# Weight sums of the seven-product pairs made ahead of the output and down projections and parked in DRAM, in a float32 decoder trunk

## Chip, cores and metric

One core of a Trainium2 chip runs the whole program. The metric is the device time of one execution in microseconds; lower is better. The engines are TensorE (PE: matmuls, with its weight loads as PEld), VectorE (DVE), ScalarE (ACT), GpSimd (POOL) and SyncE (SP); DMA transfers are issued on the queues of SP, ACT and POOL.

## What is computed

256 tokens of width 2048 go through two decoder layers in float32. The first layer mixes tokens by gated linear attention with four heads, the second by causal attention with 16 heads over one shared key and value; a gated feed-forward with a short convolution follows each. Cut to what matters:

```python
# layer 0
q, k, v, g = split(rms_norm(x) @ w_in)                       # 2048 -> 1024, 1024, 2048, 2048
h = x + (rms_norm(gla(q, k, v, decay)) * silu(g)) @ gla_w_out      # "go": 2048 x 2048
# each layer's feed-forward
a, u = split(causal_conv3(rms_norm(h) @ w_up) + conv_b)            # "up": 2048 x 11264
h = h + (silu(a) * u) @ w_down                                     # "dn": 5632 x 2048
# layer 1
k, v = split(rms_norm(h) @ kv_w);  q = rms_norm(h) @ w_q           # "kk", "kv", "mq"
h = h + softmax_attention(q, k, v, rel_bias) @ moba_w_out          # "mo": 2048 x 2048
```

All weights together are some 411 MB of float32, each read once.

## The kernel before

**Products in three parts.** A float32 product is made of three matmuls: each operand is split into a rounded high part and a low part (`whi`, `wlo` of the weights), and high x high, high x low and low x high are accumulated. So each weight piece of 128x1024 is cast by ScalarE (`whi`, line 132) and subtracted by VectorE (`wlo`, line 133) before TensorE can use it.

**The weight stream.** `WeightStream` holds all weights in the order of use as chunks of 128x2048 (1 MiB), each read by one DMA on SP's queue into one of three raw buffers (`wraw`, line 95), and as halves of 128x1024. A step of the program takes one half (`step`, `get`); `prefetch` splits two to five halves ahead, into three pairs of buffers with some more from a pool of 34 general slots. A raw buffer is free for the chunk three later when its last split is done. Jobs beside the stream are queued with `after(steps, job)` and run when that step comes. From the code so recorded a scheduler, which models the engines in time, sets the order of each engine's instructions; every engine then works its own list strictly in order.

**Projections.** `gemm_tok` makes 512 columns for 256 tokens in eight steps of twelve matmuls (lines 281 and 284). The results come out tokens by features; where features by tokens are needed, `turned` (attention) and the feed-forward's `store` and `load` write the tile to DRAM and read it back turned, on POOL's queue, and jobs some steps later use it: 6 and 7 steps after for keys, queries and gates, 6 and 8 for the convolution (`convolve`).

**Output and down projections.** `down` serves go, dn0, mo and dn1. Each works in two column groups of 1024, over pairs k of 256 input rows (8 in go and mo, 22 in dn). A pair is a 2x2 block product. Done plainly it takes eight block products, so 24 matmuls in two steps. A seven-product pair (marked `+` in `ORDERS`) takes seven, so 21 matmuls in four steps, with sums of the input blocks (`combine`, `combs`) and of the weight blocks. Those weight sums, tiles `t` of two times 128x1024, are made by `_sums` on VectorE when the pair's chunk has come, and then split like any other half:

```python
        V.tensor_sub(t13, src[:, 512:1536], src[:, 0:1024])
        V.tensor_add(t24[:, :512], t13[:, 512:], src[:, :512])
        V.tensor_sub(t24[:, 512:], src[:, 1536:], t24[:, :512])
```

Pairs behind the `|` in `ORDERS` form the tail of a column group: they are run once for each half of its columns. After the last seven-product pair the partial sums are gathered (`c`, lines 718 to 722), four accumulating DMAs add the old rows to them (`c<-x_tok`, `c<-rows`, line 724), and after each half of the tail VectorE adds the tail's products (line 733). Finished blocks are stored, and turned by TensorE transposes (`back`, line 757) into the next stage's operand `xw`; `TURNS` says in which tail pair.

41 pairs are seven-product pairs: 4 in go, 16 in dn0, 4 in mo, 17 in dn1.

Of the kernel before, what the change touches and what calls it, by code (L numbers as in the profile page):

```python
# [27 lines left out]
FT = F // 128  # L28
# [9 lines left out]
def _order(text):  # L38
# [7 lines left out]
    "go": [_order("0 1+ 2 3+ 4 | 5 6 7"), _order("0 2 1+ 3+ 4 | 5 6 7")],  # L46
    "dn0": [_order("0 2 4 6 1+ 8 3+ 10 5+ 12 7+ 14 9+ 16 11+ 17 13+ 18 15+ | 19 20 21"),
            _order("0 2 4 6 1+ 8 3+ 10 5+ 12 7+ 14 9+ 16 11+ 17 13+ 18 15+ 19 | 20 21")],
    "mo": [_order("0 2 1+ 3+ 4 | 5 6 7"), _order("0 2 1+ 3+ 4 | 5 6 7")],
    "dn1": [_order("0 2 4 6 1+ 8 3+ 10 5+ 12 7+ 14 9+ 16 11+ 17 13+ 18 15+ | 19 20 21"),  # L50
            _order("0 1+ 2 3+ 4 5+ 6 7+ 8 9+ 10 11+ 12 13+ 14 15+ 16 17+ 18 | 19 20 21")],
# [3 lines left out]
TURNS = ((0, (1, 2)), (0, (1, 2)), (1, (0, 1)), (1, (0, 1)), (1, (1, 2)), (1, (1, 2)))  # L55


class WeightStream:
# [4 lines left out]
    def __init__(self, tc, raw, parts):  # L63
# [4 lines left out]
        self.cuts, self.lead, self.deep = {}, {}, set()  # L68
        self.sums, self.slot, self.first = {}, None, None

    def add(self, w, g, cols):
        for c0 in range(0, cols, 2048):
            n = min(2048, cols - c0)
            for o in range(0, n, 1024):
                self.halves.append((len(self.chunks), o, "plain"))
            self.chunks.append((w, g, c0, n))

    def add_quads(self, w, g, order, deep):

        first = len(self.halves)  # L80
        for i, (_, seven) in enumerate(order[0]):
            c = len(self.chunks)
            self.halves += ([(c, 0, "b11"), (c, 1024, "wide"), (c, 0, "t13"), (c, 0, "t24")] if seven else
                            [(c, 0, "wide"), (c, 1024, "wide")])
            self.chunks.append((w, g, 2048 * i, 2048))
        if deep:
            self.deep.update(range(first, len(self.halves)))

    def _dma(self, upto):
        while self.n_dma < min(upto, len(self.chunks)):  # L90
            w, g, c0, n = self.chunks[self.n_dma]
            t = self.raw.tile([128, 2048], F32, name="wraw")
            for a, b in self.cuts.get(self.n_dma, ((0, n),)):
                rows = w[g, 128 * c0:128 * (c0 + n)].rearrange("(p c) -> p c", p=128)
# [6 lines left out]
    def _sums(self, c):  # L101

        V, src = self.nc.vector, self.tiles[c]
        t13, t24 = (self.slot([128, 1024], F32, k) for k in ("t13", "t24"))
# [5 lines left out]
    def prefetch(self, i):  # L110
        nc = self.nc
        while self.n_split < len(self.halves):
# [10 lines left out]
            if kind == "b11":  # L123
                src = src[:, :512]
# [938 lines left out]
```

## Time and profile before

| | us |
|---|---|
| median of 3 runs | 2235.65 (2232.77 to 2240.84) |
| the profiled execution | 2234.8 |
| its span, first to last instruction | 2233.0 |
| TensorE busy | 2192.9 (98%), 9805 matmuls |
| VectorE busy | 1585.1 (71%) |
| ScalarE busy | 1270.8 (57%) |
| GpSimd busy | 263.0 (12%) |
| DMA | 495.40 MB, mean 222 GB/s |

By the first matmul of each stage the attention projections run to 297 us of the span, go to 405, the first up projection to 885, dn0 to 1122, the cross projections (mq, kk, kv) to 1420, mo to 1512, the second up projection to 1992, and dn1 to the end. Matmuls are pipelined and one is counted as busy from its issue to its modelled end; how fast TensorE goes is seen better from the number of matmuls in a stretch than from its busy time. A line of code such as 132 or 692 serves many tiles, so rows name the tile too.

### The profile page before, as it was taken

The numbers are of one execution on the slowest core, as the hardware profiler recorded it, in microseconds if no ns is written. First come the engines' busy times: TensorE is split into PE (matmuls) and PEld (weight loads), VectorE is DVE, ScalarE is ACT, GpSimd is POOL, SyncE is SP. The second block draws the span as 40 slices with busy tenths as digits, with TensorE's granted clock in tenths as the row PEclk, the third lists the DMA queues.
The fourth block names the chain that finished last, engine by engine and source line by source line (L and its number), as shares of the span: only waits on it lengthen the run. The fifth ranks groups of instructions, "written<-read, shape, count | busy, mean of one in ns | idle before, by whom it ended". The sixth has DMA issues, their size and how long they took to land.

```text
span 2233.0 us, 26994 instructions
## 1 busy us (share of the span) xinstructions
PE 2192.9 (98%) x9805; PEld 1810.5 (81%) x9805; DVE 1585.1 (71%) x2162; ACT 1270.8 (57%) x1812; POOL 263.0 (12%) x368
## 2 busy tenths in 40 slices
PE   9999979999999999999999999999999999999999
PEld 7887857888888888788878888888888888887887
DVE  6655568577767767978856666776676767779886
ACT  6555545565655656555556666555565565655453
POOL 1011111111111111000021000011111111110000
PEclk9999999999999999999999999999999999999999
DMA  8576657777777787566685444486777777774655
GB/s 315 172 224 188 205 173 247 214 242 240 244 243 242 234 249 235 192 220 215 225 284 207 172 169 170 171 253 209 250 238 238 245 242 244 235 241 186 219 215 169
DMA packets 87238, 495.40 MB, mean 222 GB/s; under 512 B 12433, under 2 KB 12961, under 8 KB 37058
## 3 DMA queue, kind: packets, MB, share of 16 engines
q1 hardware_dynamic: 60578, 417.53, 53.9%
q0 software_dynamic: 25952, 75.59, 13.3%
q8 instruction: 76, 1.25, 0.2%
q10 hardware_dynamic: 576, 0.58, 0.1%
q14 instruction: 56, 0.46, 0.1%
HBM read 455.88 MB, written 37.77 MB: 221 GB/s over the span
## 4 chain that ended last, share of the span: by engine, by line
PE 82%; issue 12%; DMA 4%; DVE 1%; POOL 1%; ACT 0%; SPq 0%; DVEq 0%; POOLq 0%; ACTq 0%
PE acc L281 41%; PE acc L284 21%; PE acc L692 11%; PE p L692 7%; DMA c<-rows 1%; DMA wraw<-w_go 1%; DMA turned<-z 1%; DVE wlo L133 1%; POOL upT L634 0%; DMA turned<-queries 0%; PE sT L526 0%; PE o L543 0%; DMA wraw<-w_v 0%; DMA turned<-gates 0%; PE tr L849 0%
## 5 line engine op out<-in xcount | busy, mean ns | idle before, releaser
L133 DVE TENSOR_TENSOR wlo<-wraw,whi 128x1024 fp32r<-128x1024 f32 (+1 forms) x786 | 929.0, 1191 | 458.9 <-ACT whi L132 440.2
L132 ACT CAST whi<-wraw 128x1024 fp32r<-128x1024 f32 (+1 forms) x786 | 799.6, 1027 | 688.5 <-PE acc L281 435.3
L281 PE MATMUL acc<-whi,xw 128*128 128x512 f32 x3840 | 953.7, 390 | 3.6 <-ACT xw L244 1.9
L281 PEld LDWEIGHTS acc<-whi,xw 128*128 128x128 f32 x3840 | 720.8, 188 | 154.7 <-ACT xw L244 3.0
L284 PE MATMUL acc<-wlo,xw 128*128 128x512 f32 x1920 | 514.9, 389 | 0.0
L284 PEld LDWEIGHTS acc<-wlo,xw 128*128 128x128 f32 x1920 | 360.2, 188 | 74.7
L692 PE MATMUL acc<-whi,hid 128*128 128x512 f32 x572 | 185.2, 393 | 2.5 <-DVE c L733 2.5
L692 PE MATMUL p<-whi,hid 128*128 128x512 f32 x506 | 167.5, 393 | 0.0
L281 PE MATMUL acc<-whi,xkv 128*128 128x512 f32 x512 | 133.9, 394 | 0.0
L634 POOL DMA_DIRECT2D upT<-turned x176 | 114.0, 654 | 147.1 <-DMA turned<-z 64.5
L692 PE MATMUL acc<-whi,comb 128*128 128x512 f32 x328 | 109.2, 397 | 20.8 <-ACT whi L132 16.6
L692 PEld LDWEIGHTS acc<-whi,hid 128*128 128x128 f32 x572 | 108.2, 190 | 26.0 <-DVE c L733 3.4
L132 ACT CAST whi<-t 128x1024 fp32r<-128x1024 f32 x82 | 85.3, 1051 | 76.6 <-PE p L692 41.5
L628 POOL DMA_DIRECT2D turned<-z x44 | 34.1, 774 | 679.1 <-DVE z L624 633.0
L133 DVE TENSOR_TENSOR wlo<-t,whi 128x1024 fp32r<-128x1024 f32 x82 | 99.4, 1219 | 19.8 <-PE p L692 9.9
L692 PEld LDWEIGHTS p<-whi,hid 128*128 128x128 f32 x506 | 96.2, 190 | 20.3
L281 PEld LDWEIGHTS acc<-whi,xkv 128*128 128x128 f32 x512 | 94.1, 188 | 18.3
L642 ACT ACTIVATE au<-upT,cs 128x256 f32<-128x256 f32 x176 | 96.0, 595 | 15.8 <-DMA upT<-turned 15.7
L692 PE MATMUL acc<-wlo,hid 128*128 128x512 f32 x286 | 94.8, 390 | 0.0
L692 PEld LDWEIGHTS acc<-whi,comb 128*128 128x128 f32 x328 | 62.5, 191 | 35.9 <-ACT whi L132 18.4
L692 PE MATMUL p<-wlo,hid 128*128 128x512 f32 x253 | 83.8, 390 | 0.0
L724 POOL DMA_DIRECT2D c<-rows x24 | 21.3, 1100 | 520.1 <-DVE c L719 508.2
(241 smaller groups left out, 1931.2 us busy)
## 6 DMA issues: line engine op xcount, KB each, us to landing
wraw<-w_up SPq DMA_DIRECT2D x176, 1024.0 KB, 5.3
wraw<-w_dn SPq DMA_DIRECT2D x88, 1024.0 KB, 5.2
turned<-z POOLq DMA_DIRECT2D x44, 512.0 KB, 3.5
upT<-turned POOLq DMA_DIRECT2D x176, 128.0 KB, 4.9
wraw<-w_g SPq DMA_DIRECT2D x16, 1024.0 KB, 5.1
wraw<-w_go SPq DMA_DIRECT2D x16, 1024.0 KB, 6.1
wraw<-w_mq SPq DMA_DIRECT2D x16, 1024.0 KB, 6.1
wraw<-w_kk SPq DMA_DIRECT2D x16, 1024.0 KB, 4.9
```

Of the source, the lines that this page charges most:

```text
L132: nc.scalar.copy(hi[:, a:b], src[:, a:b])
L133: nc.vector.tensor_sub(lo[:, a:b], src[:, a:b], hi[:, a:b].bitcast(F32))
L281: T.matmul(ps[:, t, :], xs(kt)[:, x0 + 128 * t:x0 + 128 * t + 128], hi[:, c:c + 512], start=kt == 0 and x0 == 0, stop=False)
L284: T.matmul(ps[:, t, :], xs(kt)[:, 128 * t:128 * t + 128], lo[:, c:c + 512], start=False, stop=kt == KT - 1)
L628: nc.gpsimd.dma_start(turned[J].rearrange("(a i) r q c -> (i r) a (q c)", a=4), z.rearrange("p (a q) t c -> p a (q t c)", a=4))
L634: nc.gpsimd.dma_start(f[32 * q:32 * q + 32].rearrange("p a (i c) -> p (a i) c", i=4), turned[J][:, :, q, :].rearrange("a r c -> r a c"))
L642: A.activation(au[:, i, :], t[:, i, :], AF.Identity, bias=col(cb + n), scale=col(cw + 2 * 2 * FT + n))
L692: T.matmul(p[n], x[xi], w[wi][:, 512 * f:512 * f + 512], start=n not in begun, stop=left[n] == 0)
L724: nc.gpsimd.dma_start(r[n], res(n // 2, 2 * b + n % 2), accum_op=OP.add)
```

## The change

The weight sums are no longer made in the output and down projections. While the projections run, `make_sums` starts, every few steps, a job that fetches a later chunk of a seven-product pair a second time, on POOL's queue in two halves into two general slots; four steps later VectorE makes four sums of 128x512 in place, and POOL's queue parks them in DRAM. In the down stages a seven-product pair then reads two chunks, the raw one (its halves `b11` and `wide`) and the parked sums. 14 sums are made in the attention projections (every 5 steps), 10 in the first part of each up projection (every 8), 14 in the cross projections (every 6). With that the seven-product pairs become 48: 6 in go, 18 in dn0, 6 in mo, 18 in dn1. The orders of pairs are new, and go and mo have a tail of two pairs, not three, right behind a seven-product pair.

Jobs on turned tiles, and the sums, are recorded inside `behind()`: they stand after the latest weight split on ScalarE and VectorE. The turned tiles are used one or two steps later than before.

```diff
-    "go": [_order("0 1+ 2 3+ 4 | 5 6 7"), _order("0 2 1+ 3+ 4 | 5 6 7")],
+    "go": [_order("0 2 1+ 4 3+ 5+ | 6 7"), _order("0 2 1+ 4 3+ 5+ | 6 7")],
...
-TURNS = ((0, (1, 2)), (0, (1, 2)), (1, (0, 1)), (1, (0, 1)), (1, (1, 2)), (1, (1, 2)))
+TURNS = ((0, (1, 1)), (0, (1, 1)), (1, (0, 1)), (1, (0, 1)), (1, (1, 1)), (1, (1, 1)))
...
+            self.cuts[c] = ((0, 512), (1024, 2048))
+            sums = self.parked([128, 2048])
+            self._add(sums, 2048)
+            self.unmade.append((rows, sums))
+            self.halves += [(c, 0, "b11"), (c, 1024, "wide"), (c + 1, 0, "wide"), (c + 1, 1024, "wide")]
...
-    def _sums(self, c):
...
+    def behind(self):
+        stack = ExitStack()
+        for ins in self.latest:
+            stack.enter_context(self.tc.issue_after(ins))
+        return stack
+    def fetch_blocks(self):
+        rows, sums = self.unmade.pop(0)
+        x = [self.slot([128, 1024], F32, "sums") for _ in range(2)]
+        for i in range(2):
+            self.nc.gpsimd.dma_start(x[i], rows[:, 1024 * i:1024 * i + 1024])
+        def make():
+            V = self.nc.vector
+            (b11, b12), (b22, b21) = ((t[:, :512], t[:, 512:]) for t in x)
+            with self.behind():
+                V.tensor_sub(b11, b12, b11)
+                V.tensor_sub(b12, b22, b12)
+                V.tensor_sub(b22, b22, b11)
+                V.tensor_sub(b21, b21, b22)
+            for i in range(2):
+                self.nc.gpsimd.dma_start(sums[:, 1024 * i:1024 * i + 1024], x[i])
+        return make
...
+            self.latest = [one.ins, two.ins]
...
+    def make_sums(first, count, every):
+        for i in range(count):
+            def fetch():
+                job = ws.fetch_blocks()
+                after(4, job)
+            after(first + every * i, fetch)
...
+    make_sums(24, 14, 5)
...
-        through(hd, z, [(6 + i, lambda f, c=2 * hd + i: gated(c, f)) for i in range(2)])
+        through(hd, z, [(8 + i, lambda f, c=2 * hd + i: gated(c, f)) for i in range(2)])
...
+        make_sums(2, 10, 8)
...
-                after(6 + 2 * i, lambda J=J, i=i: convolve(2 * J + i, f[J][:, 2 * i:2 * i + 2, :]))
+                after(8 + 2 * i, lambda J=J, i=i: convolve(2 * J + i, f[J][:, 2 * i:2 * i + 2, :]))
...
+    make_sums(4, 14, 6)
```

`ws.cuts` is assigned anew further down, in both kernels, so the entry for the shorter load is not in force.

What the scheduler makes of it, at three places. First ScalarE at the start of go, before; `g<-turned` (now L619) is the job on a turned gate tile, `tok<-acc` (now L630) the evacuation of the last gate projection:

```order
L132 CAST whi<-t_2307 128x1024
L132 CAST whi<-wraw 128x1024
L589 ACTIVATE g<-turned,cs 128x256 x4
L600 ACTIVATE tok<-acc,col_n 128x512 x2
L294 CAST go<-g 128x2x256
```

and after:

```order
L151 CAST whi<-wraw 128x1024 x2
L630 ACTIVATE tok<-acc,col_n 128x512 x2
L151 CAST whi<-wraw 128x1024 x2
L151 CAST whi<-wraw 128x512
L151 CAST whi<-wraw 128x1024 x2
L619 ACTIVATE g<-turned,cs 128x256 x4
L312 CAST go<-g 128x2x256 x2
```

The evacuation has moved ahead of the turned tile, with five weight pieces between them.

Second VectorE near the start of dn0, before; `t` are weight sums, `comb` and `whole` sums of inputs, `au` belongs to the convolution:

```order
L105 TENSOR_TENSOR t_7148<-wraw 128x1024
L571 TENSOR_TENSOR comb<-whole,comb 128x128
L133 TENSOR_TENSOR wlo<-wraw,whi 128x512
L649 TENSOR_TENSOR au<-au 128x256
L568 TENSOR_TENSOR comb<-whole 128x128
L570 TENSOR_TENSOR comb<-whole 128x128
L578 TENSOR_TENSOR whole<-hid 128x512
L106 TENSOR_TENSOR t_7149<-t_7148,wraw 128x512
L133 TENSOR_TENSOR wlo<-t_7148,whi 128x1024
```

and after, from the low part of a pair's last sums on:

```order
L152 TENSOR_TENSOR wlo<-wraw,whi 128x1024 x3
L152 TENSOR_TENSOR wlo<-wraw,whi 128x512
L608 TENSOR_TENSOR whole<-hid 128x512
L598 TENSOR_TENSOR comb<-whole 128x128
L600 TENSOR_TENSOR comb<-whole 128x128
L677 SCALAR_TENSOR_TENSOR au<-upT,cs,au 128x255
L152 TENSOR_TENSOR wlo<-wraw,whi 128x1024
```

The sums are gone from among the splits; the input sums and the convolution are still there.

Third TensorE at the end of go's first column group, before; `p_2409` is a product of the tail's second half of columns, `c_2572` and `c_2574` are finished row blocks that are transposed:

```order
L692 MATMUL p_2409<-whi,go 128x512 x4
L692 MATMUL p_2409<-wlo,go 128x512 x2
L692 MATMUL acc<-whi,go 128x512 x4
L692 MATMUL acc<-wlo,go 128x512 x2
L692 MATMUL acc<-whi,go 128x512 x4
L692 MATMUL acc<-wlo,go 128x512 x2
L757 MATMUL acc<-mk,c_2572 128x2x2x32
L757 MATMUL acc<-mk,c_2574 128x2x2x32
```

and after, where `p_2567` is that product, `c_2837` and `c_2839` are those blocks and `p_2960` belongs to the next group:

```order
L726 MATMUL p_2567<-wlo,go 128x512 x2
L726 MATMUL acc<-whi,go 128x512 x4
L726 MATMUL acc<-wlo,go 128x512 x2
L791 MATMUL acc<-mk,c_2837 128x2x2x32
L726 MATMUL acc<-whi,go 128x512 x4
L726 MATMUL acc<-wlo,go 128x512 x2
L726 MATMUL acc<-whi,go 128x512 x4
L726 MATMUL acc<-wlo,go 128x512 x2
L726 MATMUL acc<-whi,go 128x512 x4
L726 MATMUL acc<-wlo,go 128x512 x2
L726 MATMUL acc<-whi,go 128x512 x2
L791 MATMUL acc<-mk,c_2839 128x2x2x32
```

Between the group's last seven-product pair and its first transpose there stood an eight-product pair and most of a tail of three pairs; now there are 42 matmuls of a tail of two, and the transposes of the second block come 20 matmuls later.

More of the change, by code (lines that the diff above doesn't have):

```diff
@@ L67, in __init__, with _add @@
         self.n_dma = self.n_split = 0
-        self.cuts, self.lead, self.deep = {}, {}, set()
-        self.sums, self.slot, self.first = {}, None, None
+        self.cuts, self.lead = {}, {}
+        self.unmade, self.slot, self.parked, self.first = [], None, None, None
+        self.latest = []
+    def _add(self, rows, n):
+        self.chunks.append((rows, n))
+        return len(self.chunks) - 1
     def add(self, w, g, cols):
@@ L114, in prefetch @@
             c, o, kind = self.halves[n]
-            if n > i + self.AHEAD + (kind != "plain") + 2 * (n in self.deep):
+            if n > i + self.AHEAD + (kind != "plain"):
                 break
             self._dma(c + 1)
-            for c_, _, kind_ in self.halves[n:n + (5 if n in self.deep else 3)]:
-                if kind_ == "b11" and c_ not in self.sums:
-                    self._dma(c_ + 1)
-                    self._sums(c_)
-            src = self.sums[c][kind] if kind in ("t13", "t24") else self.tiles[c][:, o:o + 1024]
-            if kind == "b11":
-                src = src[:, :512]
-            if kind != "plain" and n % 4 == 3 or n in self.deep and n % 2:
+            src = self.tiles[c][:, o:o + (512 if kind == "b11" else 1024)]
+            if kind != "plain" and n % 4 == 3:
                 hi, lo = self.slot([128, 1024], F32R, "whi"), self.slot([128, 1024], F32R, "wlo")
@@ L177, in trunk @@
     ws = WeightStream(tc, raw, parts)
+    ws.parked = lambda shape: dram.tile(shape, F32, name=f"sums{len(ws.unmade)}")
     plan = [(w_v2, 1, 16384), (w_v, 2, 8192), (w_k, 2, 8192), (w_qa, 2, 8192), (w_g, 4, 8192), (w_go, "go", None),
@@ L184, in trunk @@
             for g, order in enumerate(ORDERS[groups]):
-                ws.add_quads(w, g, order, groups in ("go", "mo"))
+                ws.add_quads(w, g, order)
             continue
@@ L388, in through, with run @@
             after(2, lambda: got.update(f=load(g)))
+            def run(job):
+                with ws.behind():
+                    job(got["f"])
             for lag, job in jobs:
-                after(lag, lambda job=job: job(got["f"]))
+                after(lag, lambda job=job: run(job))
         return square, through
@@ L639, in convolve @@
             au = temp("au")
+            with ws.behind():
+                for i in range(2):
+                    n = i * FT + j
+                    A.activation(au[:, i, :], t[:, i, :], AF.Identity, bias=col(cb + n),
+                                 scale=col(cw + 2 * 2 * FT + n))
             for i in range(2):
                 n = i * FT + j
-                A.activation(au[:, i, :], t[:, i, :], AF.Identity, bias=col(cb + n),
-                             scale=col(cw + 2 * 2 * FT + n))
                 V.scalar_tensor_tensor(au[:, i, 1:], t[:, i, :S - 1], col(cw + 2 * FT + n), au[:, i, 1:],
```

54 lines of the change are left out of this document (21 added, 33 removed).

## Prediction

> **What bounds the kernel now.** I read the page's busy shares first, then the span in stretches of 50 us.
>
> ```profile
> span 2233.0 us, 26994 instructions
> PE 2192.9 (98%) x9805; PEld 1810.5 (81%) x9805; DVE 1585.1 (71%) x2162; ACT 1270.8 (57%) x1812; POOL 263.0 (12%) x368
> ```
>
> ```profile
> 150.00:200.00 50.00, 47.27 (x206) 39.20 (x205) 26.35 (x35) 20.84 (x27) 8.03 (x10) 0.93 0.75 216
> 300.00:350.00 50.00, 33.82 (x132) 26.38 (x132) 28.92 (x33) 22.91 (x32) 7.58 (x9) 0.86 0.55 163
> 900.00:950.00 50.00, 45.70 (x187) 36.29 (x186) 48.00 (x74) 28.57 (x37) 0.00 (x0) 0.93 0.47 171
> 1700.00:1750.00 50.00, 50.00 (x223) 41.40 (x222) 34.64 (x51) 29.59 (x42) 6.72 (x10) 1.00 0.77 249
> 2000.00:2050.00 50.00, 45.86 (x189) 36.50 (x188) 47.83 (x75) 26.94 (x37) 2.29 (x4) 0.93 0.55 191
> ```
>
> The columns are PE, PEld, DVE, ACT and POOL busy with their counts, the granted clock, the DMA share and GB/s. TensorE is the bound nearly everywhere: an undisturbed stretch (1700) holds 222 to 223 matmuls, 0.225 us each, a step of twelve 2.70 us. The count shows what the busy time hides, since matmuls at a lowered clock also count as busy: 300:350 is 90 matmuls short (20.3 us), 900:950 is 35 short (7.9 us), 2000:2050 33 short (7.4 us). These three are the start of the attention output product ("go") and of the two down projections. So a change can gain by fewer matmuls, or in these three places. The go start, in order of time:
>
> ```profile
> 305.55 1.70 ACT L589 ACTIVATE g<-turned,cs 128x256 f32<-128x256 f32 x4 [5.09 <-DMA turned<-gates]
> 307.16 1.24 ACT L600 ACTIVATE tok<-acc,col_n 128x512 f32<-128x512 f32 x2
> 308.45 1.20 PE L692 MATMUL acc<-whi,comb 128*128 128x512 f32 x4 [4.14 <-ACT tok L600]
> 327.37 1.04 ACT L132 CAST whi<-wraw 128x1024 fp32r<-128x1024 f32 x1 [7.97 <-DMA wraw<-w_go]
> 333.09 1.04 ACT L132 CAST whi<-wraw 128x1024 fp32r<-128x1024 f32 x1 [4.67 <-DMA wraw<-w_go]
> 337.25 0.80 PE L692 MATMUL acc<-whi,comb 128*128 128x512 f32 x1 [10.86 <-ACT whi L132]
> ```
>
> ScalarE sits 5.09 us on a turned tile while the evacuation (L600) that TensorE needs stands behind it. Fifteen microseconds later two weight loads are late, and TensorE waits 10.86 us. At the down projections another engine is full:
>
> ```profile
> 920.00:925.00 5.00, 1.67 (x5) 0.59 (x4) 5.00 (x10) 1.60 (x2) 0.00 (x0) 0.89 0.00 0
> 925.00:930.00 5.00, 4.46 (x11) 3.49 (x12) 5.00 (x8) 4.15 (x6) 0.00 (x0) 0.50 0.60 210
> L105 DVE TENSOR_TENSOR t<-wraw 128x1024 f32<-128x1024 f32 x3 | 3.7, 1217 | 1.6 <-DMA wraw<-w_dn 1.6
> L106 DVE TENSOR_TENSOR t<-t,wraw 128x512 f32<-128x512 f32 x3 | 2.0, 681 | 0.0
> L107 DVE TENSOR_TENSOR t<-wraw,t 128x512 f32<-128x512 f32 x3 | 2.0, 681 | 0.0
> ```
>
> VectorE is busy for all of both stretches, DMA idle in the first. The groups (busy us, mean ns of one) are those of 885:932, where 7.7 us of VectorE's work are weight sums. After the gap the clock is 0.50.
>
> **The change, part by part.** *Products.* Seven more pairs of seven save 3 matmuls each: 21 x 0.225 = 4.7 us, on the bound. **-4.7.**
>
> *Weight sums out of the down stages.* 41 times (1.2 + 0.68 + 0.68) = 105 us of VectorE leave them, 7.7 us in each of the two places where VectorE is full. What is lost there is 7.9 and 7.4 us. The convolutions now come two steps (5.4 us) later into that stretch, so I take 7 each: **-14**, bounds -15.3 and 0.
>
> *Turned work behind the latest piece.* At the go start the evacuation now stands ahead of the turned tile and that tile's job is 2 steps later, more than the 5.09 us. The two late loads followed when ScalarE and VectorE caught up and freed raw buffers together; without the first wait, and without sums in the raw buffers, most of that goes. Against it, go loads 22 pieces instead of 16 beside the last turned tiles. I take **-14** of the 20.3; bounds -20.3 and 0.
>
> *Sums in the projections.* 48 times four subtractions of 128x512 by 0.68 us are 131 us of VectorE; 192 half-piece transfers of 0.5 MiB and 48 more piece loads of 1 MiB carry 151 MB more. The first subtraction waits on VectorE for its fetch, issued four steps (10.8 us) before; behind it stand the next splits, whose pieces TensorE needs some three steps later. (The shortened load of a seven-product piece does not come about: the table of cuts is overwritten later, and the SP order still loads 2048 columns.) By stage before, and what DMA can do:
>
> ```profile
> 65.00:297.00 232.00, 229.26 (x1042) 191.06 (x1042) 136.59 (x170) 126.77 (x181) 29.83 (x38) 0.99 0.63 199
> 405.00:621.00 216.00, 216.00 (x960) 178.97 (x959) 151.29 (x222) 126.68 (x185) 31.55 (x47) 1.00 0.74 235
> 1122.00:1420.00 298.00, 296.68 (x1436) 247.16 (x1435) 195.00 (x316) 177.98 (x308) 29.98 (x31) 1.00 0.55 193
> 292.00:296.00 4.00, 4.00 (x20) 3.30 (x19) 2.01 (x2) 0.97 (x3) 0.00 (x0) 1.00 1.01 423
> 324.00:328.00 4.00, 2.38 (x11) 1.65 (x9) 0.00 (x0) 0.63 (x1) 0.00 (x0) 1.00 1.05 280
> ```
>
> Full DMA moved 423 GB/s with weights alone and 280 with turned tiles of attention beside them. The attention projections get 14 sums (29.4 MB): 199 becomes 326 GB/s, the share 0.63 becomes 0.93, VectorE 0.59 becomes 0.75. The first 216 us of each up projection get 10 (21 MB): 235 becomes 332, 0.74 becomes 0.97, VectorE 0.70 becomes 0.83. The cross projections get 14: 0.55 becomes 0.78, VectorE 0.65 becomes 0.78. So on average it fits, hidden under matmuls. In the late half of attention it does not quite: the 150:200 row's 0.75 plus 2.1 MB per five steps (13.5 us, 155 GB/s, 0.37) is 1.12. What is late then is the software queue, and behind it on POOL the turned loads and the small pow instructions:
>
> ```profile
> POOL rr L839 <- DVE ss L837: 169.5, 8, 32.6
> ACT whi L132 <- PE acc L281: 435.3, 317, 2.4
> L634 POOL DMA_DIRECT2D upT<-turned x176 | 114.0, 654 | 147.1 <-DMA turned<-z 64.5
> upT<-turned POOLq DMA_DIRECT2D x176, 128.0 KB, 4.9
> ```
>
> Until now POOL waited before each rr; now fetches and parks stand there, each park behind its subtractions on VectorE, and VectorE waits for rr. The second row is the cover: pieces mostly wait for TensorE, not TensorE for them. Cost between 0 and 12% of 147 us (18) in attention, taken 5, since the stage's mean is below full; 0 to 8 in each up projection, taken 1 each; 0 to 18 in the cross projections (8 rr, each late by one landing of 4.9 us less a step of 2.7), taken 3, near the cover's end. **+10.** POOL's own issue, 192 by 0.65 us, lies in its 88% idle time.
>
> By the Trainium skill ("DMA: Bandwidth & Descriptors", section "Where 436 GB/s comes from") memory binds HBM transfers at about 358 GB/s for a core. An estimate by that: the late half of attention, which wants 371, runs 4% over, 5 us on the sum; the 423 row stands against it, if for 4 us only.
>
> *Loads in the down stages.* A pair of seven now needs two pieces in 21 x 0.225 = 4.7 us of products, and two pieces at 423 GB/s take 5.0; a pair of eight between (one piece in 5.4 us) gives it back. Three pairs of seven stand in a row at three places, where the DMA falls 0.9 us behind before a landing of 5 us or so is counted; so 0 to 6 us, taken near the lower end: **+2.**
>
> *The shorter tail of go and mo.* This is the new wait. Before, an eight-product pair and a tail of three followed the last seven-product pair; now a tail of two follows at once. In that time the partial sums must take in the old rows by DMA:
>
> ```profile
> 339.79 0.58 ACT L718 COPY c<-acc 128x512 f32<-128x512 f32 x1 [0.18 <-PE acc L692]
> 342.24 0.94 POOL L724 DMA_DIRECT2D c<-x_tok  x1 [19.20 <-DVE c L719]
> 352.11 0.69 DVE L733 TENSOR_TENSOR c<-c,acc 128x512 f32<-128x512 f32 x1 [1.28 <-DMA c<-x_tok]
> 357.55 0.69 DVE L733 TENSOR_TENSOR c<-c,p 128x512 f32<-128x512 f32 x1 [4.75 <-DMA c<-x_tok]
> 358.53 0.60 PE L757 MATMUL acc<-mk,c 128*128 128x128 f32 x4
> c<-rows POOLq DMA_DIRECT2D x24, 256.0 KB, 8.8
> ```
>
> The last seven ended at 339.5; the first row block was whole 13.3 us later, the second 18.7, and the transposes came at 19.0, just in time. In the new order 42 matmuls (9.5 us) stand before the first transpose of the first group and 62 (14.0 us) before the second's, and 42 and 48 (10.8) in the last group, and TensorE takes them in order. Readiness as before (13.3 and 18.7) gives waits of 3.8 + 0.9 us in a first group and 3.8 + 4.1 in a last one, 25 us over go and mo, with some half-clock time behind them 28. VectorE is freer now: with issue 1.2 us after the last product, a landing of 8.8 and the addition of 0.7, the first block is ready at 10.7 and the second some 2.5 later, and the waits are 1.2 and 2.3 us, 7 in all; a quicker landing leaves 4. Between the two, nearer the lower: **+13.**
>
> Sum: -4.7 - 14 - 14 + 10 + 2 + 13 = -7.7. The profiled execution took 2234.8 us, 0.85 below the median 2235.65; from the median **2228 us**.
>
> **Rivals.** *B, the tails stay hidden:* the scheduler's places are met, because accumulates land early in a quieter software queue. For it: 8.8 us is a median, and c<-x_tok waited only 1.28 us in the first row. Then 2228 - 13 = 2215. *C, DMA is full, slower:* with fetch, park and turned tiles mixed, DMA delivers some 300 GB/s, between the 280 row and 325. Attention needs 46.2 + 29.4 MB and each up half 50.8 + 21: 219 MB at 300 take 730 us against 664 of matmuls. Late turned tiles block ScalarE and VectorE ahead of the next pieces, and up to 66 us appear there, less the 7 counted: up to 2287; at 323 GB/s it costs 15, 8 more than counted, and the gain is gone. With half of that price, since lags of 7 and 8 steps and the slack of later stages absorb a part: 2254. *D, go stays as it is:* six more pieces beside the turned gates and the last parks, so its loads are late again: 2228 + 14 = 2242.
>
> **Chances.** Forecast 0.42 (own range 2219 to 2237), B 0.24, C 0.20, D 0.14. About 0.3% (6.7 us) is what a measurement can tell from no change. The forecast lies at that edge: 0.24 of its 0.42 counts as faster, 0.18 as the same; B faster; D half same, half slower; C slower but 0.02: faster 0.48, same 0.27, slower 0.25. For the range I cut B's better end (all bounds of gain: 2195) and C's worse half: 2207 to 2254.
>
> **What would show it.** Right: 300:350 without the wait on turned gates ahead of the evacuation, VectorE below full at the start of the down projections, TensorE waits on c in the tails of go and mo, DMA above 320 GB/s in attention at an unbroken matmul count. Wrong: turned or sums tiles as releasers of ScalarE or VectorE with TensorE waiting in the projections (C), w_go or sums pieces as releasers at go (D), no wait at the transposes (B).

## The result, and the profile after

The changed kernel takes 2266.7 us in the median (2262.5 to 2270.8), the kernel before 2234.2 beside it: a ratio of 1.0141 with a 95% interval of 1.0111 to 1.0170. It is 1.4% slower and lies above the range, where 2228 had been forecast. The profiled execution took 2266.8 us. The page's first lines:

```profile
span 2265.0 us, 27747 instructions
PE 2201.1 (97%) x9784; PEld 1805.7 (80%) x9784; DVE 1626.9 (72%) x2280; ACT 1284.0 (57%) x1834; POOL 368.3 (16%) x560
```

TensorE ran 21 matmuls fewer, as forecast, and the span is 32 us longer. The stretches that answer to those of before (columns as there: PE, PEld, DVE, ACT, POOL busy with counts, clock, DMA share, GB/s):

```profile
65.00:297.00 232.00, 227.84 (x1045) 188.49 (x1043) 161.86 (x214) 126.18 (x180) 55.64 (x85) 1.00 0.90 304
150.00:200.00 50.00, 46.87 (x203) 37.39 (x202) 38.12 (x52) 26.22 (x37) 15.19 (x24) 1.00 0.98 328
411.00:627.00 216.00, 216.00 (x955) 178.69 (x955) 169.88 (x253) 124.79 (x183) 52.71 (x86) 0.99 0.96 321
1130.00:1428.00 298.00, 294.36 (x1412) 243.92 (x1411) 217.46 (x360) 173.70 (x301) 59.64 (x85) 1.00 0.80 291
300.00:350.00 50.00, 42.69 (x167) 30.50 (x166) 39.52 (x51) 28.26 (x39) 11.98 (x16) 0.97 0.90 295
907.00:957.00 50.00, 42.32 (x173) 34.03 (x173) 38.82 (x61) 27.09 (x36) 0.00 (x0) 0.90 0.68 242
2034.00:2084.00 50.00, 43.49 (x184) 35.16 (x183) 38.47 (x60) 27.14 (x36) 0.00 (x0) 0.93 0.73 257
```

The projections (first four rows) carry the making nearly unharmed. The DMA shares of the first, third and fourth row are within 0.03 of those worked out. The late half of attention (second row), for which 1.12 had been worked out, moves 328 GB/s at a share of 0.98, and TensorE does 203 matmuls there instead of 206. The starts of the down projections (last two) have VectorE at 38 of 50 us, where 48 stood before, and still hold fewer matmuls (173 and 184; before 187 and 189). TensorE's waits, in all, times, longest (us): first two rows of the kernel before, then of the changed one.

```profile
PE acc L692 <- ACT whi L132: 16.6, 3, 10.9
PE acc L692 <- DVE c L733: 2.5, 2, 1.5
```
```profile
PE acc L726 <- ACT whi L151: 21.6, 14, 5.3
PE acc L791 <- DVE c L767: 10.7, 3, 5.5
PE acc L726 <- DVE c L767: 10.2, 4, 5.4
PE acc L726 <- DVE wlo L152: 5.1, 3, 2.4
PE hf L791 <- DVE c L767: 1.7, 1, 1.7
PE p L726 <- DVE c L767: 1.2, 1, 1.2
```

Waits for c, the output sums, grew from 2.5 to 23.8 us; waits for high parts of weights became many small ones and did not go. By stage, from the first weight matmul of one to that of the next in the trace, and in dn1 to the last one (us; "cross" is its three projections; the experiments follow below):

| kernel | attention | go | up0 | dn0 | cross | mo | up1 | dn1 |
|---|---|---|---|---|---|---|---|---|
| before | 291.7 | 107.4 | 480.1 | 237.1 | 298.1 | 91.5 | 480.1 | 237.1 |
| changed | 293.2 | 111.8 | 481.5 | 237.8 | 299.2 | 105.2 | 484.5 | 241.8 |
| e1 old tails | 290.4 | 95.4 | 480.1 | 239.0 | 297.6 | 92.1 | 480.1 | 242.4 |
| e4 no making | 286.0 | 103.1 | 480.3 | 237.8 | 298.2 | 101.9 | 481.3 | 241.2 |
| e7 e1, no making | 285.9 | 95.9 | 480.1 | 236.1 | 298.6 | 90.8 | 480.1 | 250.3 |
| e8 eight behind | 291.3 | 112.5 | 481.5 | 240.9 | 300.1 | 107.2 | 481.6 | 245.0 |
| e17 earlier making | 290.8 | 100.9 | 481.5 | 239.2 | 299.6 | 104.9 | 481.8 | 245.8 |
| e5 before, new tails | 292.0 | 99.8 | 481.5 | 236.7 | 298.5 | 98.5 | 481.4 | 235.6 |
| e9 before, "behind" | 288.7 | 99.1 | 480.1 | 237.1 | 298.3 | 91.3 | 480.1 | 236.8 |
| e15 e9, late convolutions | 286.7 | 99.1 | 480.1 | 236.6 | 298.1 | 91.5 | 480.1 | 236.1 |
| e10 e1, dn order | 291.6 | 95.1 | 480.3 | 238.6 | 298.2 | 92.8 | 480.4 | 237.0 |
| e13 e10, convolutions | 289.1 | 96.3 | 480.1 | 229.4 | 301.7 | 92.6 | 480.3 | 230.9 |
| e14 e9, four parked | 286.9 | 98.9 | 480.1 | 232.9 | 298.1 | 91.4 | 480.1 | 231.7 |

The loss lies in go and mo with what follows them, and the gain expected in dn0 and dn1 is missing. The ends of the two column groups of mo, in order of time (start, us, engine, line, operation, then in brackets the idle time before it and what ended it):

```profile
1465.34 0.57 ACT L752 COPY c<-acc 128x512 f32<-128x512 f32 x1
1467.77 0.88 POOL L758 DMA_DIRECT2D c<-rows  x1 [36.25 <-DVE c L753]
1472.08 2.63 POOL L758 DMA_DIRECT2D c<-rows  x3 [3.43 <-DVE c L755]
1477.61 0.69 DVE L767 TENSOR_TENSOR c<-c,acc 128x512 f32<-128x512 f32 x1 [3.20 <-DMA c<-rows]
1478.35 2.08 PE L726 MATMUL acc<-whi,ox 128*128 128x512 f32 x4 [5.36 <-DVE c L767]
1514.62 0.58 ACT L752 COPY c<-acc 128x512 f32<-128x512 f32 x1
1523.78 0.67 DVE L767 TENSOR_TENSOR c<-c,acc 128x512 f32<-128x512 f32 x1
1532.89 0.69 DVE L767 TENSOR_TENSOR c<-c,p 128x512 f32<-128x512 f32 x1 [4.80 <-DMA c<-rows]
1533.63 0.90 PE L791 MATMUL acc<-mk,c 128*128 128x128 f32 x3 [5.54 <-DVE c L767]
```

In the first group it is the next group's first product that waits longest (its accumulators are not yet emptied), in the last group the transposes. The first row block can be added to 9 to 12 us after the copy begins, the second only 18.

### The profile page after: what moved, and what is told of

Read it like the earlier page. It is cut to its first block, busy times and chain, and to the rows that moved or that the text cites. A ratio compares the mean times of both kernels' runs of the same rounds, so it can differ in the third digit from the quotient of the medians.

```text
span 2265.0 us, 27747 instructions
## 1 busy us (share of the span) xinstructions
PE 2201.1 (97%) x9784; PEld 1805.7 (80%) x9784; DVE 1626.9 (72%) x2280; ACT 1284.0 (57%) x1834; POOL 368.3 (16%) x560
## 5 line engine op out<-in xcount | busy, mean ns | idle before, releaser
L152 DVE TENSOR_TENSOR wlo<-wraw,whi 128x1024 fp32r<-128x1024 f32 (+1 forms) x882 | 1038.7, 1190 | 482.1 <-ACT whi L151 442.6
L151 ACT CAST whi<-wraw 128x1024 fp32r<-128x1024 f32 (+1 forms) x882 | 890.1, 1026 | 755.9 <-PE acc L299 367.7
L726 PE MATMUL p<-whi,hid 128*128 128x512 f32 x488 | 161.6, 393 | 1.2 <-DVE c L767 1.2
L726 PE MATMUL acc<-whi,comb 128*128 128x512 f32 x384 | 125.2, 397 | 7.8 <-ACT whi L151 7.5
L131 POOL DMA_DIRECT2D sums<-sums x96 | 53.0, 552 | 453.1 <-DVE sums L127 304.3
L726 PEld LDWEIGHTS acc<-whi,comb 128*128 128x128 f32 x384 | 72.5, 190 | 28.1 <-ACT whi L151 13.4
L679 DVE SCALAR_TENSOR_TENSOR au<-upT,cs,au 128x254 f32<-128x254 f32 x176 | 80.9, 476 | 0.0
```

Source lines behind the costliest of these rows:

```text
L131: self.nc.gpsimd.dma_start(sums[:, 1024 * i:1024 * i + 1024], x[i])
L151: one = nc.scalar.copy(hi[:, a:b], src[:, a:b])
L152: two = nc.vector.tensor_sub(lo[:, a:b], src[:, a:b], hi[:, a:b].bitcast(F32))
L679: V.scalar_tensor_tensor(au[:, i, 2:], t[:, i, :S - 2], col(cw + n), au[:, i, 2:], op0=OP.mult, op1=OP.add)
L726: T.matmul(p[n], x[xi], w[wi][:, 512 * f:512 * f + 512], start=n not in begun, stop=left[n] == 0)
```

## Experiments

Each time is a median, each ratio against the kernel before on the same chip.

**Old tails.** go and mo get their orders of before, with two pairs of seven fewer in each of them, so 44 sums.

```diff
-    "go": [_order("0 2 1+ 4 3+ 5+ | 6 7"), _order("0 2 1+ 4 3+ 5+ | 6 7")],
+    "go": [_order("0 1+ 2 3+ 4 | 5 6 7"), _order("0 2 1+ 3+ 4 | 5 6 7")],
...
-    make_sums(24, 14, 5)
+    make_sums(24, 12, 5)
```

> The changed kernel with the go and mo orders of before: two pairs of seven in a group, an eight-product pair and a tail of three behind the last of them (44 pairs of seven and parked sums in place of 48). Theory T (the tail is the largest loss: TensorE's waits for c grew from 2.5 to 23.8 us): they go back to about 2.5, -21.3, and 12 matmuls more cost 2.7: 2266.7 - 18.6 = 2248 us. Rival R (the additions come late because the software queue is full, whatever stands behind the last pair of seven): the waits for c stay above 15 us and the time stays within 2258 to 2268.

2231.0 us, 0.9990 (0.9976 to 1.0004): 36 us less than the changed kernel, twice what T had worked out. (Two makings fewer run in the attention and two in the cross projections.) Waits for c fell to 0.3 us. mo and up1 together gave back 17.5 us, go and up0 17.8. The first half of the first up projection beside it, with ten makings:

```profile
396.00:612.00 216.00, 216.00 (x960) 178.96 (x959) 171.13 (x251) 125.00 (x174) 50.22 (x81) 1.00 0.98 326
```

DMA at 0.98 and 326 GB/s costs TensorE not one matmul: 960, as before. What up0 and up1 had lost in the changed kernel came from the tails ahead of them.

**Sums in other buffers.** Parked sums are loaded into slot buffers, not raw ones.

```diff
+            if self.n_dma in self.parts_of:
+                t = [self.slot([128, 1024], F32, "wsum") for _ in range(2)]
+                for i in range(2):
+                    self.nc.sync.dma_start(t[i], rows[:, 1024 * i:1024 * i + 1024])
...
```

> The changed kernel with the loads of parked sums going to two slot buffers of 512 KiB instead of a raw buffer, for 41 of the 48 pairs (not the last seven pairs of the first group of dn0): the three raw buffers then hold weights alone, as before the change. Theory T (a pair of seven now takes two of the three raw buffers, so a piece is asked for too late and TensorE waits 25 us for whi and wlo at the starts of go, dn0 and dn1): half to all of these waits go, 2266.7 less 13 to 25: 2242 to 2254 us. Rival R (DMA bandwidth or VectorE holds the splits there): within 3 us of 2266.7.

2265.8 us, 1.0143 (1.0126 to 1.0161): the rival's number; T fell. At the start of dn0 the pieces were there, and the wait went to the engines that split them, VectorE with splits and convolutions and ScalarE behind it:

```profile
923.49 1.21 DVE L161 TENSOR_TENSOR wlo<-wraw,whi 128x1024 fp32r<-128x1024 f32 x1
925.19 0.42 ACT L690 ACTIVATE au<-au 128x256 f32<-128x256 f32 x1 [2.90 <-DVE au L688]
926.38 1.04 ACT L160 CAST whi<-wraw 128x1024 fp32r<-128x1024 f32 x1
927.47 1.22 PE L735 MATMUL acc<-whi,hid 128*128 128x512 f32 x2 [8.43 <-ACT whi L160]
```

**Shorter loads in force.**

```diff
-    ws.cuts = {0: ((0, 512), (512, 1024), (1024, 1536), (1536, 2048))}
+    ws.cuts[0] = ((0, 512), (512, 1024), (1024, 1536), (1536, 2048))
```

> The changed kernel with the shortened load of a seven-product piece in force (its columns 512 to 1024 are not loaded): 48 times 0.25 MiB less on the hardware queue. Theory T (the late loads are a matter of when they are asked for and how long one takes): each late piece lands about 0.6 us earlier (0.25 MiB at the 423 GB/s seen), some 10 waits, so 4 to 8 us less: about 2261 us. Rival R (DMA bytes bind in the starts of go and the down projections): 10 us or more off, 2257 or below.

2275.8 us, 1.0198 (1.0173 to 1.0224): 9 us slower than the changed kernel, which neither had. The load becomes two transfers, and no smaller one lands earlier by much (median us from issue to landing at the row's end); TensorE's waits for high parts of weights rose from 21.6 to 37.5 us:

```profile
wraw<-w_dn SPq DMA_DIRECT2D x52, 1024.0 KB, 6.2
wraw<-w_dn SPq DMA_DIRECT2D x36, 512.0 KB, 6.3
wraw<-w_dn SPq DMA_DIRECT2D x36, 256.0 KB, 5.3
```
```profile
PE acc L726 <- ACT whi L151: 37.5, 27, 4.8
```

**No making.** One parked tile serves all loads of sums.

```diff
-            sums = self.parked([128, 2048])
+            self.one = getattr(self, "one", None) or self.parked([128, 2048])
+            sums = self.one
...
-    make_sums(24, 14, 5)
+    make_sums(24, 1, 5)
```

> The changed kernel without 47 of the 48 makings: no fetch of blocks, no subtractions and no park in the projections but for one; every load of sums reads that one parked tile, so all pieces and products of the down stages stay (their values are not the reference's). Theory T (the making is nearly hidden: projections lost 8.4 us against before, and the last parks 2 or 3 at the start of go): 2266.7 - 11 = 2256 us, between 2252 and 2260. Rival R (the traffic of the making, 151 MB with its queues, is the main loss, through delayed tiles): 2235 to 2245 us.

2241.3 us, 1.0035 (1.0022 to 1.0049): 25 us less than the changed kernel, so R's number. By stage attention gave 7, go 9, mo 3 and the up projections 4 us; e17 below shows that what go gives hangs on when the last parks are issued.

**The tails alone**, in the kernel before.

```diff
-    "go": [_order("0 1+ 2 3+ 4 | 5 6 7"), _order("0 2 1+ 3+ 4 | 5 6 7")],
+    "go": [_order("0 2 1+ 4 3+ 5+ | 6 7"), _order("0 2 1+ 4 3+ 5+ | 6 7")],
...
```

> The kernel before with the new orders of go and mo alone (three pairs of seven, then at once a tail of two); its weight sums stay on VectorE in the down stages, nothing is parked. Theory T1 (the tail costs by itself: waits for c of some 20 us and half-clock time behind them, less 2.7 us of products): 2234 + 22 = 2256 us. Rival T2 (the tail hurts only beside the making's traffic in the software queue and the parked pieces' loads): 2229 to 2239 us.

2238.5 us, 1.0018 (1.0001 to 1.0034): 4 or 5 us slower than the kernel before, T2's number. Yet the profile shows the tail's price there too, mo and up1 8.3 us longer, and beside it a gain of 6.2 in go and up0: the new order of go waits less for high parts of weights at its start (8.8 us in the whole kernel, where 16.6 stood). Waits for c:

```profile
PE acc L692 <- DVE c L733: 13.9, 7, 4.5
```

**Earlier convolutions**, on e1.

```diff
-                after(8 + 2 * i, lambda J=J, i=i: convolve(2 * J + i, f[J][:, 2 * i:2 * i + 2, :]))
+                after(6 + 2 * i, lambda J=J, i=i: convolve(2 * J + i, f[J][:, 2 * i:2 * i + 2, :]))
```

> e1_tail with the convolutions of the up projections back at lags of 6 and 8 steps (8 and 10 in the change); still behind the latest piece. Theory V (VectorE is full at the starts of dn0 and dn1 because the last convolutions were moved there in place of the weight sums): waits of 8.6 and 7.3 us there and the half clock behind them go, 10 to 16 us off the 2231 of e1_tail: 2215 to 2221. Rival L (the pieces themselves come too late there): within 3 us of 2231; a second rival, that earlier convolutions make ScalarE and VectorE wait for turned tiles in the projections: above 2234.

2359.8 us, 1.0563 (1.0535 to 1.0592): the second rival, 129 us slower than e1. ScalarE now stands in front of turned tiles that have not landed (first row e6, second e1):

```profile
ACT au L673 <- DMA upT<-turned: 202.5, 42, 8.8
```
```profile
L673 ACT ACTIVATE au<-upT,cs 128x256 f32<-128x256 f32 x176 | 94.4, 595 | 2.3 <-DMA upT<-turned 2.3
```

Whether this comes from the convolution's place right behind a piece or from the making's transfers beside it was not separated; the kernel before has these lags with neither.

**No making, old tails:** e1 with the edit of e4.

```diff
-    make_sums(24, 12, 5)
+    make_sums(24, 1, 5)
...
```

> e1_tail without 43 of its 44 makings (no fetches, subtractions and parks; every load of sums reads the one parked tile, so its values are not the reference's). Theory T (with the old tails the making is almost hidden: what is left is in the attention projections and the first loads of go): 2231 - 6 = 2225, between 2221 and 2229. Rival R (the making costs as much as e4_nomake against the changed kernel, 25 us, whatever the tails): 2203 to 2210.

2228.0 us, 0.9974 (0.9956 to 0.9992): T. Beside the old tails the making costs 3 us, beside the new ones 25 (e4). The 3 us are a balance: attention is 4.5 and dn0 2.9 us shorter than in e1, dn1 7.9 longer, and no run shows why. Set against e4, this run gives the price of the new tails without the making: 19.7 us in go, up0, mo and up1 together.

**An eight-product pair behind the pairs of seven**, in the changed kernel.

```diff
-    "go": [_order("0 2 1+ 4 3+ 5+ | 6 7"), _order("0 2 1+ 4 3+ 5+ | 6 7")],
+    "go": [_order("0 2 1+ 3+ 5+ 4 | 6 7"), _order("0 2 1+ 3+ 5+ 4 | 6 7")],
```

> The changed kernel with all 48 pairs of seven, but go and mo in the order 0 2 1+ 3+ 5+ 4 | 6 7: three pairs of seven in a row and the eight-product pair 4 (24 matmuls, 5.4 us) between the last of them and the tail of two. Theory T1 (the price of the tail is the time between the last pair of seven and the end of the group): each of the four waits shrinks by up to 5.4 us and the half clock with it, 2266.7 - 18 = 2249, between 2243 and 2255. Rival L (six pieces in a row come too late): 2260 or more, the waits for whi taking the place of those for c.

2268.1 us, 1.0159 (1.0137 to 1.0181): the rival's number, though not its picture: waits for high parts rose to 25.8 us, but those for c stayed at 23.4. They only moved to later blocks. TensorE hardly waits for the first block any more (0.9 us in one group of four), 1.4 to 1.7 for the second in each group, and at the ends of go and mo the first product of the next stage waits 4.9 and 5.6 for the last. The end of mo, whose gathering begins at 1514.62:

```profile
1536.14 0.69 DVE L767 TENSOR_TENSOR c<-c,p 128x512 f32<-128x512 f32 x1 [3.23 <-DMA c<-rows]
1539.10 3.40 PE L299 MATMUL acc<-whi,xw 128*128 128x512 f32 x8 [5.59 <-DVE c L767]
```

So 5.4 us more of products cover the first of the four accumulating DMAs and not the last.

**One part of the change alone:** turned tiles of attention behind the latest piece, in the kernel before.

```diff
-                after(lag, lambda job=job: job(got["f"]))
+                after(lag, lambda job=job: run(job))   # run: with ws.behind(): job(got["f"])
...
-        through(hd, z, [(6 + i, lambda f, c=2 * hd + i: gated(c, f)) for i in range(2)])
+        through(hd, z, [(8 + i, lambda f, c=2 * hd + i: gated(c, f)) for i in range(2)])
```

> The kernel before with one part of the change: in the attention projections turned tiles are worked on behind the latest weight piece, with the new lags there (7, 8, 10, 13). Up projections, weight sums on VectorE, 41 pairs and all orders stay as before. Theory T (this part alone gives what the prediction counted for it): attention as in e4_nomake, 6 us less, and the start of go 8 to 12 less: 2233.9 - 16 = 2218, between 2214 and 2222. Rival S (the gain at go came from taking the weight sums out of it): 2227 to 2236.

2220.9 us, 0.9953 (0.9938 to 0.9969): T. Attention is 3.0 and go 8.3 us shorter.

**Order at the start of the down projections**, on e1.

```diff
-    "dn0": [_order("0 2 4 1+ 6 3+ 8 5+ 10 7+ 12 9+ 14 11+ 16 13+ 18 15+ 17 | 19 20 21"),
+    "dn0": [_order("0 2 4 6 1+ 8 3+ 10 5+ 12 7+ 14 9+ 16 11+ 17 13+ 18 15+ | 19 20 21"),
```

> e1_tail with the first groups of dn0 and dn1 in the order of before (0 2 4 6 1+ 8 3+ ... in place of 0 2 4 1+ 6 3+ ...): the same 16 pairs of seven, the first of them one eight-product pair (5.4 us) later, and a tail right behind the last. Theory V (VectorE is full there with the last convolutions and the combinations for the first pairs of seven; a later first pair spreads them): the waits of 9.3 and 7.3 us at the two starts fall by half or more, 6 to 14 off the 2231 of e1_tail: 2217 to 2225. Rival L (one late piece, whatever the order): 2228 to 2234.

2223.4 us, 0.9953 (0.9936 to 0.9970): V's number, though in this profile only dn1 is shorter, by 5.4.

**Deeper look-ahead** in go and mo, in the changed kernel.

```diff
-            if n > i + self.AHEAD + (kind != "plain"):
+            if n > i + self.AHEAD + (kind != "plain") + 2 * (n in self.deep):
```

> The changed kernel with the deeper look-ahead of before in go and mo (weights split two half-pieces further ahead, with four more slot buffers in use). Theory D (go and mo lose because the change took that depth out: pieces late at the start, and splits in the way of the additions in the tail): 2266.7 less 10 to 20: 2247 to 2257. Rival (the depth doesn't matter, the landing of the accumulating DMAs does): 2262 to 2270.

2272.2 us, 1.0178 (1.0158 to 1.0197): D fell; the rival's 2262 to 2270 was missed by 2. Go and mo are 5.6 and 7.2 us longer. (The change also takes this look-ahead out of go and mo; its description above does not mention it.)

**Rows loaded ahead**, in the changed kernel.

```diff
-                        nc.gpsimd.dma_start(r[n], res(n // 2, 2 * b + n % 2), accum_op=OP.add)
+                        V.tensor_add(r[n], r[n], old[n // 2][:, n % 2])   # old: loaded two pairs earlier
```

> The changed kernel with the old rows of go and mo loaded into two slot buffers two pairs before the last pair of seven, and added by VectorE (four additions of 0.68 us a group) in place of the accumulating DMAs: no landing of 9 us stands between the last pair of seven and the tail. Theory T (that landing sets the waits for c, 23.8 us, and the half clock behind them, 8): 2266.7 - 28 = 2239, between 2234 and 2246. Rival R (the additions themselves are late, behind splits on a full VectorE, or late pieces take their place): 2255 or more.

2253.2 us, 1.0094 (1.0079 to 1.0110): between the two. Waits for c fell from 23.8 to 9.2 us, the sum of four rows, of which the two largest:

```profile
PE acc L299 <- DVE c L775: 5.0, 2, 3.1
PE hf L799 <- DVE c L775: 2.5, 1, 2.5
```

So 13.5 us of the tail hang on the accumulating DMAs; VectorE's additions, which stand among splits, still come late.

**Convolutions back where nothing is made**, on e10 (an up projection has 22 blocks).

```diff
-            with ws.behind():
+            with ws.behind() if j < 24 else nullcontext():
...
-                after(8 + 2 * i, lambda J=J, i=i: convolve(2 * J + i, f[J][:, 2 * i:2 * i + 2, :]))
+                after((8 if J < 12 else 6) + 2 * i, lambda J=J, i=i: convolve(2 * J + i, f[J][:, 2 * i:2 * i + 2, :]))
```

> e10_dn_order with the convolutions of the second half of each up projection (from its 13th block of 24 on... that is, blocks 12 and later) as before: lags 6 and 8 and not behind the latest piece. The makings are over by then. Theory V (convolutions moved two steps later fill VectorE at the starts of dn0 and dn1): the waits of 5 and 4 us left there and their half clock go, 2223 less 6 to 9: 2214 to 2217. Rival L (pieces come late there): 2220 to 2226. Rival P (lag 6 makes ScalarE wait for turned tiles, as in e6, without any making beside it): 2235 or more.

2213.5 us, 0.9910 (0.9890 to 0.9929): V; dn0 and dn1 are 9.2 and 6.1 us shorter than in e10. (The cross projections are 3.5 longer there, which was not followed up.)

**Four sums parked** for each down projection, in e9.

```diff
+            if seven and self.quota:      # 4 in the first group of dn0 and of dn1
+                self.quota -= 1
+                sums = self.parked([128, 2048])
...
```

> e9_behind_alone with the sums of only the first four pairs of seven of dn0 and of dn1 made and parked, in the second half of the up projection before them (8 of 41; one every 14 steps); all else as in e9. Theory V (VectorE is full only at these two starts, and 7.7 us of its work there are sums): 7.9 and 7.4 us lost there fall to a third, 2221 less 8 to 12: 2209 to 2213. Rival L (the two pieces that a parked pair needs come late there instead): 2218 to 2225.

2212.1 us, 0.9898 (0.9879 to 0.9916): V, 1.0% below the kernel before and the lowest time here, though e13 (0.9910) is not told apart from it.

**Only the late convolutions**, in e9.

```diff
+            with ws.behind():
...
-                after(6 + 2 * i, lambda J=J, i=i: convolve(2 * J + i, f[J][:, 2 * i:2 * i + 2, :]))
+                after(8 + 2 * i, lambda J=J, i=i: convolve(2 * J + i, f[J][:, 2 * i:2 * i + 2, :]))
```

> e9_behind_alone with the change's move of the convolutions alone: behind the latest piece, at 8 and 10 steps, with the weight sums still on VectorE in the down stages. Theory V: 7 us more of VectorE's work come into the two starts that were full already, 2221 plus 8 to 14: 2229 to 2235. Rival L (VectorE is not what ends the waits there): 2218 to 2225.

2220.2 us, 0.9939 (0.9922 to 0.9955): V fell here; the move costs nothing where the sums are.

**A later first pair of seven in go**, in e14.

```diff
-    "go": [_order("0 1+ 2 3+ 4 | 5 6 7"),
+    "go": [_order("0 2 1+ 3+ 4 | 5 6 7"),
```

> e14_park_four with the first group of go in the order 0 2 1+ 3+ 4 instead of 0 1+ 2 3+ 4: the first pair of seven one eight-product pair later. Theory G (the wait of 7.9 us for a late w_go piece at the start of go hangs on sums and splits being asked for at once there): half of it and its half clock go, 4 to 7 below e14. Rival: within 3 of e14.

2218.2 us, 0.9924 (0.9907 to 0.9941): 6 us slower than e14; G fell, go is 7.3 us longer.

**Makings 8 steps earlier**, in the changed kernel.

```diff
-    make_sums(24, 14, 5)
+    make_sums(16, 14, 5)
```

> The changed kernel with the 14 makings of the attention projections begun 8 steps earlier (step 16 instead of 24, still one every 5 steps), so that the last park ends some 20 us before go starts. Theory P (in the changed kernel the last parks stand in the way of go's first loads of sums and of its last turned tiles): 2266.7 less 6 to 10: 2257 to 2261. Rival T (go loses by its tails and its third pair of seven alone): 2264 to 2270.

2252.4 us, 1.0087 (1.0066 to 1.0108): 14 us less than the changed kernel, more than P had. In the profiled executions, which differ by 10.5, go is 10.9 us shorter and attention 2.4, and dn1 4.0 longer. In the changed kernel three parks are issued by POOL after go has begun, and the first parked piece is late (rows of POOL, ScalarE and TensorE in order of time); in e17 the last park is issued at 287:

```profile
299.83 0.54 POOL L131 DMA_DIRECT2D sums<-sums  x1 [3.21 <-DVE sums L129]
308.09 0.57 POOL L131 DMA_DIRECT2D sums<-sums  x1 [2.55 <-DVE sums L127]
309.54 0.55 POOL L131 DMA_DIRECT2D sums<-sums  x1 [0.89 <-DVE sums L129]
313.68 1.04 ACT L151 CAST whi<-wraw 128x1024 fp32r<-128x1024 f32 x1 [6.83 <-DMA wraw<-sums]
314.78 1.65 PE L726 MATMUL acc<-whi,comb 128*128 128x512 f32 x3 [2.65 <-ACT whi L151]
```
```profile
287.47 0.54 POOL L131 DMA_DIRECT2D sums<-sums  x1 [0.80 <-DVE sums L129]
```

**All four remedies with 48 pairs and the new tails** (e12, e10, e13, e17 together).

> The changed kernel with its 48 pairs and its new tails of go and mo, and four remedies: rows loaded ahead (as e12), first groups of dn0 and dn1 in the order of before (as e10), convolutions of the second half of the up projections as before (as e13), makings of attention 8 steps earlier (as e17). If the causes add up: 2266.7 - 13.5 (e12) - 17.5 (e1 to e13) - 0 to 8 = 2228 to 2236. Rival (they share one cause, or the tails keep the price that e1 showed): 2240 or more; below 2220 would say that the tails cost nothing once their landing is gone.

2224.8 us, 0.9964 (0.9950 to 0.9979): 42 us less than the changed kernel, 3 below the range for causes that add up. Together the remedies take back all of the loss and 9 us more, and still it is 13 us behind e14 with its 41 pairs.

## Why the prediction was wrong

Between the forecast and the result lie 40 us. With each term of the sum put into the stage where it belongs, and the tail's 13 halved between go and mo, 19 of them are in dn0 and dn1 (forecast 14.0 us shorter, measured 5.4 longer), 14 in go and up0 (7.9 shorter, 5.8 longer) and 12 in mo and up1 (6.2 longer, 18.1 longer); attention and cross lost 5 less than forecast.

*The shorter tail (+13) was mis-sized, and is the largest loss.* e1 gives 36 us, but it also took two makings out of the attention projections, and ending those earlier is worth up to 14 (e17); what is left is about 22, or 24 with the 2.7 us of products given back. That they add was not run by itself, but e4 against e7, with one making each, agrees with 19.7 us, or 22 with the products. So do the waits for c, 21.3 us more.

The step that failed was "VectorE is freer now", and in it the second block, "some 2.5 later" than the first. Counted from the start of the copy, which came 0.1 to 2.3 us after the pair's last product, the first block was whole after 10.0, 9.5, 13.0 and 9.9 us in the four groups of go and mo, near the 10.7 forecast but for one. The second was whole after 18.5, 17.6, 18.9 and 19.0. VectorE's additions stand between splits, so the first accumulating DMA left 2.4 us after the copy began and the other three only after 5.9 to 7.8, and VectorE waited for a landing until 16.9 to 18.3. That is the old readiness of the second block (18.7), from which the prediction had worked out 25 to 28 and which it then did not take; the value nearer the lower bound rested on no row of such a tail. It had also looked for the wait at the transposes alone; in the first groups the next group's first product waits as well.

In the kernel before, the same tail costs 8.3 us in mo and up1 (e5), or 9.7 with the products, where half of the forecast is 6.5. There, in the two groups of mo, the other three accumulating DMAs left from 3.4 and 5.3 us on, and the second block was whole after 11.7 and 16.5. What makes it quicker than in the changed kernel was not separated; the making does not, since e4 without it shows the changed kernel's times.

*Weight sums out of the down stages (-14): right in size, wrong in its condition.* The prediction saw that the convolutions come two steps later and discounted 1.3 us in all for it (14 where 15.3 was lost). Four combinations (e9, e15, e10, e13) show that it takes the whole gain. At the start of dn0, the second and third 15 us; first the kernel before (sums there, convolutions early, as in e9), then e15 (both there), e10 (late convolutions alone), e13 (neither):

```profile
899.80:914.80 15.00, 15.00 (x68) 12.38 (x66) 15.00 (x30) 9.30 (x14) 0.00 (x0) 1.00 0.48 158
914.80:929.80 15.00, 10.70 (x35) 7.47 (x34) 15.00 (x26) 8.38 (x11) 0.00 (x0) 0.80 0.36 135
```
```profile
886.40:901.40 15.00, 14.38 (x64) 11.58 (x62) 15.00 (x27) 9.44 (x14) 0.00 (x0) 1.00 0.45 159
901.40:916.40 15.00, 11.28 (x40) 8.29 (x41) 15.00 (x27) 8.77 (x12) 0.00 (x0) 0.89 0.33 124
```
```profile
887.30:902.30 15.00, 14.05 (x62) 11.33 (x61) 12.05 (x23) 8.74 (x14) 0.00 (x0) 1.00 0.44 155
902.30:917.30 15.00, 11.65 (x45) 9.19 (x45) 13.58 (x26) 9.54 (x13) 0.00 (x0) 0.89 0.69 256
```
```profile
885.90:900.90 15.00, 14.00 (x62) 11.28 (x61) 11.52 (x24) 10.05 (x15) 0.00 (x0) 1.00 0.47 151
900.90:915.90 15.00, 13.90 (x60) 10.73 (x59) 14.39 (x26) 8.08 (x10) 0.00 (x0) 1.00 0.87 322
```

The second row of each pair holds 35, 40, 45 and then 60 matmuls; dn0 and dn1 together take 473.9, 472.7, 475.6 and 460.3 us. Either load alone keeps the wait, and only without both it goes, 13.6 us, of which 2.5 are 11 matmuls fewer. The four are not one kernel with two switches: e9 and e15 are built on the kernel before, e10 and e13 on the changed one. But e14, on the first base, agrees: with early convolutions, four parked sums at each start take 9.3 us off dn0 and dn1. In e10 VectorE is no longer full for all of the stretch, which suggests that the late convolutions hold the splits by their place as well as by their amount; which of the two counts more stays open. In the changed kernel dn0 and dn1 became 0.7 and 4.7 us longer instead of 14 shorter, and the order of the first pairs of seven had its part (e10).

*Turned work behind the latest piece (-14): right in the main.* Alone it is worth about 11 us (e9: 2232.2 less 2220.9), 3.0 of them in attention; one late weight load stays at the start of go in e9, with a wait of 7.5 us. In the changed kernel the wait for turned tiles ahead of the evacuation is gone, as foretold, and the stretch 300:350 holds 167 matmuls instead of 132:

```profile
299.59 1.25 ACT L630 ACTIVATE tok<-acc,col_n 128x512 f32<-128x512 f32 x2
314.63 1.70 ACT L619 ACTIVATE g<-turned,cs 128x256 f32<-128x256 f32 x4
```

What the tails and the last parks cost in go is more than this gain.

*Sums in the projections (+10): right inside the projections, wrong at their end.* The up projections lose nothing to the making (e1), the cross projections 1 us, attention 2 to 5 against e9 and 4 to 7 against e14 and e15, which treat it alike (e17 and the changed kernel). But the last makings of attention ran into the start of go, and go gives most of what e17 gains. The sum had a price for each stage's inside and none for the place where two stages meet.

*Loads in the down stages (+2)* were not separated from the rest of dn0 and dn1. e2 shows that the raw buffers do not bind there; e3 had fewer bytes but more transfers, so whether bytes bind stays open.

*The rivals.* B is refuted: the tails did not stay hidden. C's upper bound (2287) takes in the measured time, but by another mechanism: in the first half of the first up projection DMA ran at 0.98 with all 960 matmuls done (e1), and the tails account for the 955 of the changed kernel. D is near to what go did, through parks as well as pieces.

*The 5 us estimated for attention.* The Trainium skill ("DMA: Bandwidth & Descriptors", section "Where 436 GB/s comes from") gives about 358 GB/s as what memory lets through to a core. By that figure attention had been estimated to lose 5 us. The changed kernel moves 397 GB/s for 20 us in a row with 90 matmuls done, as many as undisturbed, so the figure does not bind here:

```profile
100.00:120.00 20.00, 20.00 (x90) 16.57 (x89) 14.42 (x17) 9.17 (x10) 1.60 (x3) 1.00 1.01 397
```

## What to carry to other kernels

Taking one of two loads off a full stretch can gain nothing while the other stays or moves in: test them two by two. Work that is hidden inside a stage must also end well before the next stage begins (e17). When a tail needs several transfers, count to the landing of the last one: here four were issued over some 5 us, and the last two landed 17 to 20 us after the gathering began, so that 5.4 us more of products behind the last input did not help (e8). Where a sum has two readings, the one that a row shows goes before the one that is hoped for. The version with the lowest time moves the fewest things: eight sums of 41, only where VectorE was full, and turned tiles that wait behind the weight pieces.

## What was not expected of the hardware

A load of 256 KB took 5.3 us to land and one of 512 KB 6.3, where the whole piece of 1 MiB took 6.2: cutting a quarter off a piece by splitting it in two made the kernel 9 us slower (e3). Moving the convolutions by two steps changed the time by 129 us beside the making (e6) and by nothing that can be told in e9 (e15), and nothing in the average shares of before shows that edge. DMA could be 0.98 busy for 216 us with TensorE undisturbed (e1).
